# Two convolution tiles more as TensorE products, their shifted copies by way of main memory, and the convolution's projections ahead of the index scores

## The chip, the cores and the metric

The kernel runs on one core of a Trainium2 chip. The metric is the device time of one launch in microseconds (us). Engines are named as the profile names them: PE is TensorE (PEld its weight loads), DVE is VectorE, ACT is ScalarE, POOL is GpSimd, SP issues DMAs. Each runs its own stream of instructions in order and meets the others at semaphores.

## The reference, cut to what matters

The program has a first block of two layers and a second block. Only the first block's code changes. One of its layers is

```python
proj = jnp.einsum('bld,de->ble', h, w_in[l])
a, g, zc, q, k, v, za, qi, ki, wi = jnp.split(proj, IN_SPLITS, axis=-1)
y_conv = conformer_conv_branch(a, g, zc, ...)      # u = a * sigmoid(g); depthwise conv of 31 taps;
                                                   # layer norm; silu; times silu(zc)
y_attn = dsa_sparse_attention(rope(q), rope(k), v, rope(qi), rope(ki), wi, topk) * silu(za)
h = layer_norm(alpha * h + concat(y_conv, y_attn) @ w_out[l])
```

The sequence has 512 positions and 16 meta tokens in front (528 in all), the model 1024 features, and the convolution 512 channels. The sparse attention first makes an index score of every query with every key: the relu of eight heads' dot products, weighted and added up. Of each query's scores it keeps the 132 largest (a quarter of 528), and attends to those keys alone. The second block (windowed attention, gated linear attention, 16 experts) follows on the first block's output.

## The kernel before, in words

**Tiles.** A projection tile makes 128 output features for all positions: 48 matmuls of 264 columns (eight slices of the model, three products of high and low halves, two column halves) into a PSUM tile `pp` with two buffers. ACT makes the high half of the weights (`wh`, L160), DVE the low half (`wl`, L161). The convolution's channels are four tiles c = 0 to 3. `p_ag(c)` projects a and g of such a tile, ACT makes the tanh (`th`, L363), and DVE multiplies and adds into `u` (L364).

**Two ways to do the 31 taps of a tile.** A tile in `pconv` goes tap by tap: ACT multiplies the shifted `u` by a channel's weight into `prod` (L325, two buffers), and POOL adds it to `cv` (L327). Any other tile goes through `conv_products`: PE builds a table of the taps, DVE spreads it into the weights `cwt` (L339), 16 DMAs of SP copy `u`, shifted by 0 to 3 positions, into two SBUF buffers `us` (L344), and PE then does 128 matmuls of 32 rows (two bursts, L253 and L259) into a `pp` tile, which ACT moves to `cv`. Before, layer 0 has tiles 0, 1 and 2 tap by tap and 3 as products; layer 1 has 0 and 1 tap by tap and 2 and 3 as products.

**Scores and top-k.** `p_scores` has PE make the dot products (`pidx`, L242 and L243), ACT the relu (`rl`, L424), and DVE the weighted sums (`acc`, L428): 32 for each layer, of 128 to 512 columns. Top-k is DVE's alone: for three of the four query tiles it finds the eight largest of each row (MAX8, L440) and strikes them out (MATCH_REPLACE8, L441), 17 rounds a tile. The result is a mask that attention adds to its scores (`smb`, L624). The tag `rl` has three buffers, which `rl` and `th` share. The tag `sm` has two, which `us` and `smb` share.

**What sets the order.** Every phase is emitted at a priority level. `self.plan` holds for each layer the levels from first to last, the order of the phases (`seq`) and `pconv`. A scheduler with a timeline of its own turns this into one fixed stream for each engine when the program is built. Nothing is reordered on the chip.

Of the kernel before, what the change touches and what calls it, by code (L numbers as in the profile page):

```python
# [8 lines left out]
F32 = mybir.dt.float32  # L9
# [13 lines left out]
L = S + NM  # L23
KT = D // 128
W31 = 31
PAD = W31
CQ = 4
# [42 lines left out]
class Net:  # L70
    def __init__(self, tc, I, out, dbg=None, upto=99):
        self.tc, self.nc, self.I, self.out, self.dbg = tc, tc.nc, I, out, dbg
        self.upto = upto
        self.bgq = []
        self.plan = [
            (('w', 'topk', 'tail', 'idx', 'proj', 'conv', 'att', 'ag', 'rest', 'fill'),
             ('ag0', 'idx', 'q', 'k', 'sc', 'v', 'ag2', 'ag3', 'topk', 'ag1', 'zc', 'att', 'za'),
             (2, 0, 1, 3),
             (2, 3, 1, 0),
             (0, 1, 2)),  # L80
            (('w', 'tail', 'idx', 'conv', 'proj', 'att', 'ag', 'topk', 'rest', 'fill'),
             ('idx', 'q', 'k', 'sc', 'ag1', 'v', 'ag0', 'ag3', 'topk', 'ag2', 'att', 'za', 'zc'),
             (2, 0, 1, 3),
             (2, 3, 1, 0),
             (0, 1)),
        ]
        self.order2 = ('w', 'crit', 'att', 'gla', 'main', 'late', 'fill')
        self.gn0, self.apull, self.gpull, self.ng = 2, 3, (1, 0, 2, 1), 0
        self.early = ("qk", "qk", "u", "szc", "cv", "qi", "xl", "xl", "parts", "v", "c1", "sm", "sm", "one", "raw", "raw", "raw", "hw", "hl")
        self.last = ("raw", "u", "szc", "qi")  # L90
        self.cycle = ("qk", "qk", "u", "szc", "cv", "qi", "xl", "xl", "v", "sm", "sm", "one", "raw", "raw", "raw", "hw", "hl")
        self.piece = 264
        self.swap = True
        self.stack = True
        self.sqsum, self.sqe, self.xlp = 'v', 'AAAAAAAA', ()
        self.pairs2 = False
        self.pairs, self.spare = False, None
        self.cur = None
        self.pos = 0
# [173 lines left out]
    def layer(self, l):  # L273
        nc, I = self.nc, self.I
        w_in, w_out = I["w_in"][l], I["w_out"][l]
        hT = self.hT
        q0 = 0 if l == 0 else NM
        T = L - q0
# [7 lines left out]
        order, seq, tseq, sseq, pconv = self.plan[l]  # L286
# [27 lines left out]
        u = self.sb([128, 4, PAD + L], "u")  # L314
# [5 lines left out]
        def conv_tap(c, j):  # L320
            src = u[:, c, j + 1 + q0:j + 1 + q0 + T]
            if not prod:
                prod.append(self.sb([128, 2, L], "prod", "zM"))
            pr = prod[0][:, j % 2, :T] if j else cv[:, c, :]
            nc.scalar.activation(pr, src, AF.Identity, scale=taps[:, c, j + 1:j + 2], bias=0.0 if j else cvec[:, c, 31:32])  # L325
            if j:
                nc.gpsimd.tensor_tensor(cv[:, c, :], cv[:, c, :], pr, op=ALU.add)  # L327

        def conv_products(c):
            n = T // 2
            nx = T + W31 + 1 - CQ
            pt = self.ps([128, 4, 8], "pcv")
            for g in range(4):
                for k in range(CQ):
                    nc.tensor.matmul(pt[32 * k:32 * k + 32, g, :], self.ident[:, 32 * g:32 * g + 32], taps[:, c, k::CQ], start=True, stop=True)
            w = self.sb([128, 4, 8, 32], "cwt", "k2l")
            nc.vector.tensor_tensor(w.rearrange("p g e c -> p (g e) c"), self.mask32[:, None, :].to_broadcast([128, 32, 32]),  # L339
                                    pt.rearrange("p g e -> p (g e)")[:, :, None].to_broadcast([128, 32, 32]), op=ALU.mult)  # L340
            us = [self.sb([128, 2, nx], "us", "sm", 2) for _ in range(2)]
            for g in range(4):
                for k in range(CQ):
                    nc.sync.dma_start(us[g // 2][32 * k:32 * k + 32, g % 2, :], u[32 * g:32 * g + 32, c, k + q0:k + q0 + nx])  # L344
            ps = self.ps([128, 2, 512], "pp", "pp", 2)
            for k in range(2):
                products = []
                for e in range(8):
                    for g in (3, 2, 1, 0):
                        x0 = CQ * e + n * k  # L350
                        products.append(((ps[32 * g:32 * g + 32, k, :n], w[:, g, e, :], us[g // 2][:, g % 2, x0:x0 + n]),
                                         dict(start=e == 0, stop=e == 7, skip_group_check=True)))
                self.burst(products)
            nc.scalar.activation(cv[:, c, :].rearrange("p (k n) -> p k n", k=2), ps[:, :, :n], AF.Identity, scale=1.0, bias=cvec[:, c, 31:32])

        def p_ag(c):
            self.go("ag")
            ps = []
            for n in ("a", "g"):
                raw = self.load_w(w_in, WCOL[n] + 128 * c, 128)  # L360
                ps.append(self.proj(self.split_w(raw), 128, hT, KT, fsegs))
            th = self.sb([128, L], "th", "rl", 3)
            nc.scalar.activation(fseg(th), ps[1], AF.Tanh, scale=0.5)  # L363
            nc.vector.scalar_tensor_tensor(fseg(u[:, c, PAD:]), fseg(th), 1.0, ps[0], op0=ALU.add, op1=ALU.mult)  # L364
            self.go("conv")
            if c not in pconv:
                conv_products(c)
                return
            for j in range(W31):
                conv_tap(c, j)  # L370

# [110 lines left out]
        v = self.sb([128, 4, 512], "v")  # L482
# [195 lines left out]
        def p_zc():  # L678
            self.go("rest")
            for e, ps in self.proj_tiles(w_in, WCOL["zc"], 512, hT, KT, qsegs):  # L680
                tmp = self.sb([128, T], "th", "rl", 3)
                self.silu2(seg(szc[:, e, :]), ps, seg(tmp))

        phases = dict(ag0=lambda: p_ag(0), ag1=lambda: p_ag(1), ag2=lambda: p_ag(2), ag3=lambda: p_ag(3), idx=p_idx, sc=p_scores, topk=p_topk, k=p_k, q=p_q, v=p_v, att=p_att, za=p_za, zc=p_zc)
        for n in seq:
            phases[n]()

# [12 lines left out]
        for t in range(nt):  # L700
            ps = self.ps([128, 512], "tp")
            for c in range(4):
                nc.tensor.transpose(ps[:tw, c * 128:(c + 1) * 128], cv[:, c, t * tw:(t + 1) * tw], self.ident)
            x = self.sb([128, 512], "xct", "pT" if t < 4 else "rl", 4 if t < 4 else 3)
# [56 lines left out]
        sc = self.sb([128, 5, 2], "sc")  # L761
# [1007 lines left out]
```

## Time and profile before

| | us |
|---|---|
| median of 3 runs (lowest, highest) | 1878.74 (1877.99, 1878.78) |
| profiled execution, its time | 1881.06 |
| profiled execution, its span | 1879.3 |
| PE busy | 1692.2 |
| DVE busy | 928.1 |
| ACT busy | 773.4 |
| POOL busy | 221.1 |

The span is the trace's own length. The time of the same execution holds 1.8 us more, which lies outside the trace. Layer 0 runs from the start to about 400 us, layer 1 to about 785 us, and the second block from there on. All stretches below are counted from the start of the span.

### The profile page before, as it was taken

What the parts mean: (1) busy time and instruction counts of PE and PEld (TensorE: products, weight loads), DVE (VectorE), ACT (ScalarE), POOL (GpSimd) and SP (SyncE); (2) the same over time, 40 slices, a digit from 0 to 9 for tenths busy, and PEclk for the clock granted to TensorE, in tenths of its full rate; (3) what the DMA queues carried; (4) which work ended last, traced back from release to release, by engine and by line L of the source; (5) the groups of instructions that cost most, each with busy time, mean ns of one, the idle gap of its engine ahead of it and who ended that gap; (6) DMA issues with size and microseconds to landing.
All of it is one profiled execution on the core that took longest, in us unless ns stands there. A gap on an engine that the chain in (4) does not pass through costs nothing.

```text
span 1879.3 us, 29068 instructions
## 1 busy us (share of the span) xinstructions
PE 1692.2 (90%) x11947; PEld 1343.8 (72%) x11947; DVE 928.1 (49%) x1860; ACT 773.4 (41%) x1320; POOL 221.1 (12%) x161
## 2 busy tenths in 40 slices
PE   6989699889996698899999999999899998888888
PEld 6989598879985697889988889999633332233246
DVE  3899655567993246686533446543502221022054
ACT  3874576457665346445454544322300000000036
POOL 1621771000089000000000000000000000000000
PEclk9989899889997899999998999999899999999999
DMA  6213211122222211232202337656799999999971
GB/s 191 68 46 91 58 58 46 30 70 67 68 79 73 66 46 39 62 112 78 70 23 85 92 113 249 194 175 231 267 421 420 420 420 421 421 420 420 419 279 46
DMA packets 149414, 326.79 MB, mean 174 GB/s; under 512 B 13802, under 2 KB 103594, under 8 KB 130976
## 3 DMA queue, kind: packets, MB, share of 16 engines
q1 hardware_dynamic: 144416, 313.89, 45.4%
q10 hardware_dynamic: 3856, 7.37, 1.1%
q0 software_dynamic: 1008, 3.67, 0.5%
q8 instruction: 94, 1.54, 0.3%
q14 instruction: 40, 0.33, 0.1%
HBM read 305.22 MB, written 16.25 MB: 171 GB/s over the span
## 4 chain that ended last, share of the span: by engine, by line
PE 65%; DMA 15%; DVE 10%; ACT 5%; issue 2%; POOL 1%; SPq 1%; ACTq 0%; DVEq 0%; POOLq 0%
PE pp L182 39%; PE pp L1619 8%; DMA rawe<-in_w_exp_gate 6%; DMA rawe<-in_w_exp_down 5%; DMA rawe<-in_w_exp_up 4%; PE pp L1679 2%; DVE wl L161 2%; POOL cv L327 1%; SPq L344 1%; PE pp L259 1%; DVE acc L441 1%; PE tp L594 1%; PE pidx L253 1%; PE po L253 1%; DVE m L440 1%
## 5 line engine op out<-in xcount | busy, mean ns | idle before, releaser
L327 POOL TENSOR_TENSOR cv<-cv,prod 128x528 f32<-128x528 f32 (+1 forms) x150 | 214.2, 1428 | 396.6 <-ACT prod L325 387.8
L1619 PE MATMUL pp<-rawe,xf 128*64 128x512 f32 x1024 | 248.1, 600 | 14.1 <-DMA rawe<-in_w_exp_gate 9.6
L160 ACT CAST wh<-raw 128x1024 fp32r<-128x1024 f32 (+2 forms) x149 | 151.0, 1017 | 241.4 <-PE pp L182 216.0
L182 PE MATMUL pp<-hTh,wh 128*128 128x264 f32 (+2 forms) x1056 | 225.4, 291 | 18.2 <-ACT th L363 7.3
L161 DVE TENSOR_TENSOR wl<-raw,wh 128x1024 fp32r<-128x1024 f32 (+2 forms) x149 | 187.3, 1257 | 91.5 <-ACT wh L160 85.1
L182 PE MATMUL pp<-hTl,wh 128*128 128x264 f32 (+2 forms) x1056 | 220.8, 289 | 0.0
L182 PE MATMUL pp<-hTh,wl 128*128 128x264 f32 (+2 forms) x1056 | 219.7, 287 | 0.0
L1619 PEld LDWEIGHTS pp<-rawe,xf 128*64 128x64 f32 x1024 | 78.5, 137 | 158.5 <-issue 128.5
L182 PEld LDWEIGHTS pp<-hTh,wh 128*128 128x128 f32 (+1 forms) x1056 | 166.7, 190 | 25.7 <-ACT th L363 9.3
L182 PEld LDWEIGHTS pp<-hTl,wh 128*128 128x128 f32 (+1 forms) x1056 | 165.9, 190 | 4.4 <-issue 3.7
L182 PEld LDWEIGHTS pp<-hTh,wl 128*128 128x128 f32 (+1 forms) x1056 | 165.9, 190 | 2.8 <-issue 2.4
L182 PE MATMUL pp<-xTh,wh 128*128 128x264 f32 (+1 forms) x752 | 154.3, 286 | 2.9 <-ACT op L1048 2.3
L182 PE MATMUL pp<-xTl,wh 128*128 128x264 f32 (+1 forms) x752 | 155.8, 286 | 0.8 <-DVE xTl L1143 0.8
L182 PE MATMUL pp<-xTh,wl 128*128 128x264 f32 (+1 forms) x752 | 155.3, 284 | 0.0
L1619 PE MATMUL pp<-rawe,hid 128*64 128x512 f32 x512 | 126.4, 609 | 19.4 <-DMA rawe<-in_w_exp_down 19.0
L325 ACT ACTIVATE prod<-u,taps 128x528 f32<-128x528 f32 (+1 forms) x150 | 107.7, 729 | 57.2 <-POOL cv L327 55.6
L1476 POOL DMA_INDIRECT xr<-xrows,slots x7 | 6.7, 961 | 1037.1 <-DVE xf L1456 742.0
L1508 DVE SCALAR_TENSOR_TENSOR Y<-pp,per,Y 128x512 fp32r<-128x512 f32 x16 | 12.0, 749 | 233.2 <-ACT Y L1507 233.2
L182 PEld LDWEIGHTS pp<-xTh,wh 128*128 128x128 f32 (+1 forms) x752 | 115.7, 190 | 4.6 <-ACT op L1048 2.5
L182 PEld LDWEIGHTS pp<-xTl,wh 128*128 128x128 f32 (+1 forms) x752 | 115.8, 190 | 4.2 <-issue 3.0
L182 PEld LDWEIGHTS pp<-xTh,wl 128*128 128x128 f32 (+1 forms) x752 | 116.0, 190 | 0.8 <-issue 0.8
L1619 PEld LDWEIGHTS pp<-rawe,hid 128*64 128x64 f32 x512 | 39.1, 140 | 100.7 <-issue 61.6
(515 smaller groups left out, 2933.1 us busy)
## 6 DMA issues: line engine op xcount, KB each, us to landing
rawe<-in_w_exp_gate SPq DMA_DIRECT2D x53, 1024.0 KB, 16.2
rawe<-in_w_exp_up SPq DMA_DIRECT2D x52, 1024.0 KB, 15.0
rawe<-in_w_exp_down SPq DMA_DIRECT2D x51, 1024.0 KB, 19.5
raw<-in_w_in SPq DMA_DIRECT2D x45, 1024.0 KB, 5.4
rawe<-in_w_exp_down SPq DMA_DIRECT2D x26, 512.0 KB, 15.6
rawe<-in_w_exp_up SPq DMA_DIRECT2D x22, 512.0 KB, 16.4
rawe<-in_w_exp_gate SPq DMA_DIRECT2D x22, 512.0 KB, 17.3
raw<-in_w_in SPq DMA_DIRECT2D x20, 512.0 KB, 5.1
```

The source lines that it names most:

```text
L160: nc.scalar.copy(wh, raw_view)
L161: nc.vector.tensor_sub(wl, raw_view, wh.bitcast(F32))
L182: nc.tensor.matmul(ps[:m, s, x:min(x + k, n)], a[:, t, :m], b[:, c0 + x:min(c0 + x + k, c1)], start=(t == 0 and pi == 0 and x == 0), stop= ...
L253: first = self.nc.tensor.matmul(*args, **kw)
L259: self.nc.tensor.matmul(*args, **kw)
L325: nc.scalar.activation(pr, src, AF.Identity, scale=taps[:, c, j + 1:j + 2], bias=0.0 if j else cvec[:, c, 31:32])
L327: nc.gpsimd.tensor_tensor(cv[:, c, :], cv[:, c, :], pr, op=ALU.add)
L344: nc.sync.dma_start(us[g // 2][32 * k:32 * k + 32, g % 2, :], u[32 * g:32 * g + 32, c, k + q0:k + q0 + nx])
L440: nc.vector.max(m8, acc)
L441: nc.vector.match_replace(acc, m8, acc, NEG_MARK)
L1619: nc.tensor.matmul(ps[a, s, :], x[:, a], r, start=(t == 0 and k == 0), stop=(t == KT - 2 and k == 1), skip_group_check=True)
L1679: nc.tensor.matmul(ps[k][:, k, :], a[:, t, :], wp[t][:, w, k * 512:(k + 1) * 512], start=(t == 0 and pi == 0), stop=(t == KT - 1 and pi == 2))
```

## The change

`conv_products` is cut in two. `conv_operands`, which `p_ag` calls right behind `u`, makes the weights `cwt`, copies the tile's `u` to a tensor `ud` in main memory with one DMA, and reads it back with eight DMAs (one for each column half and shift) into `us`, of which each buffer now holds one column half of all channels. `conv_products` keeps the matmuls, as phases of their own (`cp1`, `cp2`, `cp3`) at the level of the projections. `pconv` loses one tile in each layer, so that 90 taps go tap by tap (150 before), and five of the eight tiles are products (three before). In layer 0 the phase `ag3` moves ahead of the scores, `ag1` behind them, and `ag2` to just ahead of `cp2`. In layer 1 `ag2` and `ag0` move ahead of the scores.

```diff
-             ('ag0', 'idx', 'q', 'k', 'sc', 'v', 'ag2', 'ag3', 'topk', 'ag1', 'zc', 'att', 'za'),
+             ('ag0', 'idx', 'q', 'k', 'ag3', 'sc', 'ag1', 'v', 'cp3', 'ag2', 'cp2', 'topk', 'zc', 'att', 'za'),
...
-             (0, 1, 2)),
+             (0, 1)),
...
-             ('idx', 'q', 'k', 'sc', 'ag1', 'v', 'ag0', 'ag3', 'topk', 'ag2', 'att', 'za', 'zc'),
+             ('idx', 'q', 'k', 'ag2', 'ag0', 'sc', 'cp2', 'ag1', 'v', 'cp1', 'ag3', 'cp3', 'topk', 'att', 'za', 'zc'),
...
-             (0, 1)),
+             (0,)),
...
+        def conv_operands(c):
             n = T // 2
-            nx = T + W31 + 1 - CQ
+            nx = n + W31 + 1 - CQ
...
-            us = [self.sb([128, 2, nx], "us", "sm", 2) for _ in range(2)]
-            for g in range(4):
+            us = [self.sb([128, 4, nx], "us", "sm", 2) for _ in range(2)]
+            ud = self.dram.tile([128, PAD + L], F32, name=f"ud{l}{c}")
+            nc.sync.dma_start(ud, u[:, c, :])
+            for h in range(2):
                 for k in range(CQ):
-                    nc.sync.dma_start(us[g // 2][32 * k:32 * k + 32, g % 2, :], u[32 * g:32 * g + 32, c, k + q0:k + q0 + nx])
+                    x0 = k + q0 + n * h
+                    nc.sync.dma_start(us[h][32 * k:32 * k + 32], ud.rearrange("(g p) x -> p g x", g=4)[:, :, x0:x0 + nx])
+            ready[c] = w, us
+
+        def conv_products(c):
+            self.go("proj")
+            n = T // 2
+            w, us = ready.pop(c)
...
         def p_ag(c):
-            self.go("ag")
+            self.go("ag" if c in pconv else "proj")
...
+            if c not in pconv:
+                conv_operands(c)
+                return
             self.go("conv")
-            if c not in pconv:
-                conv_products(c)
-                return
```

The order that the scheduler makes of it is shown at three places. The first is DVE in layer 0, where the first score sums (`acc<-rl`) stand. Before, they stand between the rope rows (`qk`, `sw`) of the q and k tiles:

```order
L217 TENSOR_TENSOR qk<-pp,c_72 128x528
L218 TENSOR_TENSOR sw<-sw,c_72 128x528
L414 TENSOR_TENSOR rm<-rm,ws 128x128
L219 TENSOR_TENSOR qk<-qk,sw 128x528
L415 TENSOR_REDUCE acc<-rm 128x16
L428 SCALAR_TENSOR_TENSOR acc<-rl,ws,c_72 128x384
L428 SCALAR_TENSOR_TENSOR acc<-rl,ws,acc 128x384
L161 TENSOR_TENSOR wl<-raw,wh 128x1024
```

Now the last rope stands ahead of all of them, and so do the weights and the `u` (L375) of tile c = 3:

```order
L217 TENSOR_TENSOR qk<-pp,c_72 128x528
L218 TENSOR_TENSOR sw<-sw,c_72 128x528
L219 TENSOR_TENSOR qk<-qk,sw 128x528
L161 TENSOR_TENSOR wl<-raw,wh 128x1024 x2
L375 SCALAR_TENSOR_TENSOR u<-th,pp 128x528
L439 SCALAR_TENSOR_TENSOR acc<-rl,ws,c_72 128x384
L439 SCALAR_TENSOR_TENSOR acc<-rl,ws,acc 128x384 x7
```

The score sums have moved behind the k tiles that were still to come and the two projection tiles of c = 3. Layer 1 is alike: there the `u` of tiles 2 and 0 stand ahead of the first `acc`.

The second place is the end of layer 0's top-k on DVE, where the `u` of the last product tile (c = 2) now stands. Rows L451 and L452 are the rounds of top-k:

```order
L161 TENSOR_TENSOR wl<-raw,wh 128x1024
L451 MAX m_2373<-acc 128x8
L375 SCALAR_TENSOR_TENSOR u<-th,pp 128x528
L452 MATCH_REPLACE acc<-m_2336,acc 128x276
L560 TENSOR_REDUCE mxm<-smm 16x8
L452 MATCH_REPLACE acc<-m_2373,acc 128x532
L451 MAX m_2336<-acc 128x8
```

It stands behind 45 of the 51 rounds. SP issues that tile's copies behind it; the store waits for DVE, and the first load waits for the store and, with its buffer, for PE:

```order
L345 DMA ud_2207<-u 128x559 [waits DMAHW5_49,DVE_49]
L349 DMA us<-ud_2207 32x4x292 [waits DMAHW6_49,DMAHW5_49,PE_49]
L349 DMA us<-ud_2207 32x4x292 [waits DMAHW7_49]
L349 DMA us<-ud_2207 32x4x292 [waits DMAHW0_49]
L349 DMA us<-ud_2207 32x4x292 [waits DMAHW1_49]
L349 DMA us<-ud_2207 32x4x292 [waits DMAHW2_49,PE_49]
```

One store and eight loads stand where 16 copies stood. The third place is PE at the same point of layer 0:

```order
L571 MATMUL po<-vM,ptm_2655 16x512
L586 MATMUL psm<-kmb,qk 128x32 x4
L253 MATMUL pidx<-qk 128x384
L259 MATMUL pidx<-qk 128x384
L253 MATMUL pp<-us,cwt 32x264
L259 MATMUL pp<-us,cwt 32x264 x31
L253 MATMUL pidx<-qk 128x384
L259 MATMUL pidx<-qk 128x384
L605 MATMUL tp<-base,smb 128x128 x6
L182 MATMUL pp<-hTh,wh 128x264 x2
```

(The two bursts of `pp<-us` read alike; the second is left out.) The products of c = 2 are the last work ahead of attention, and all projection tiles but those of zc and za have been moved ahead of them. Before, the two tiles of `ag1` stood behind the products too. The streams of the second block are nearly the same in both programs.

## Rows read from the trace of the kernel before

**Rows 1.** Waits of PE, 0 to 330 us: total, times, longest.

```profile
PE pp L253 <- ACT prod L325: 15.4, 1, 15.4
PE pp L182 <- DVE qk L217: 6.4, 2, 5.0
```

**Rows 2.** Waits of PE, 480 to 700 us.

```profile
PE pp L253 <- DMA us<-u: 32.3, 2, 17.9
PE pp L182 <- ACT th L363: 5.9, 2, 3.0
```

**Rows 3.** Windows: length, busy of PE, PEld, DVE, ACT, POOL, granted clock, DMA.

```profile
81.40:130.00 48.60, 42.78 (x297) 41.43 (x297) 47.99 (x69) 37.13 (x66) 19.48 (x12) 0.89 0.15 44
130.00:196.60 66.60, 65.35 (x539) 60.96 (x537) 63.87 (x167) 30.07 (x51) 12.24 (x9) 1.00 0.32 88
196.60:212.00 15.40, 0.00 (x0) 0.00 (x0) 14.53 (x35) 9.21 (x13) 13.07 (x10) 0.59 0.31 74
212.00:221.50 9.50, 9.46 (x129) 8.36 (x129) 1.21 (x1) 4.54 (x7) 8.95 (x8) 0.77 0.01 2
221.50:313.00 91.50, 90.73 (x796) 82.52 (x794) 47.74 (x138) 68.06 (x144) 48.18 (x35) 1.00 0.18 59
440.00:499.30 59.30, 59.30 (x477) 58.63 (x476) 55.60 (x106) 44.61 (x78) 0.00 (x0) 1.00 0.22 63
499.30:511.00 11.70, 10.87 (x90) 10.66 (x88) 11.26 (x30) 5.15 (x11) 0.00 (x0) 1.00 0.17 46
571.30:589.20 17.90, 0.01 (x1) 0.04 (x2) 6.17 (x5) 10.21 (x15) 16.86 (x13) 0.60 0.45 126
612.30:626.60 14.30, 0.00 (x0) 0.00 (x0) 1.84 (x2) 1.32 (x2) 0.00 (x0) 0.62 0.41 105
626.60:635.10 8.50, 8.44 (x128) 7.50 (x128) 0.00 (x0) 0.00 (x0) 0.00 (x0) 0.84 0.02 4
635.10:712.00 76.90, 76.90 (x702) 70.13 (x699) 37.22 (x129) 41.24 (x102) 0.00 (x0) 1.00 0.17 56
```

**Rows 4.** Timeline of DVE, 84 to 85 us and 199 to 222 us.

```profile
84.03 1.39 DVE L428 SCALAR_TENSOR_TENSOR acc<-rl,ws,c 128x384 f32<-128x384 f32 x1
...
199.65 0.69 DVE L364 SCALAR_TENSOR_TENSOR u<-th,pp 128x528 f32<-128x528 f32 x1
...
206.43 0.09 DVE L441 MATCH_VALUE_LOAD acc<-m,acc 128x8 f32 x1
...
208.49 0.09 DVE L441 MATCH_VALUE_LOAD acc<-m,acc 128x8 f32 x1
...
221.58 0.62 DVE L624 CUSTOM_DVE_ANT_0 smb<-pidx,acc,mi 128x384 f32<-128x384 f32 x1 [8.37 <-PE pp L259]
```

**Rows 5.** Timeline of SP, 199 to 222 us: start, length, what it issues.

```profile
200.37 10.01 SPq L344 DMA_DIRECT2D us<-u  x16
```

**Rows 6.** The tile `us`: time from issue to landing of its DMAs.

```profile
DMA to landing us min/median/max: 2.0/2.0/2.0
```

**Rows 7.** Timeline of DVE in layer 1: first sum, and the `u` behind top-k.

```profile
451.67 0.61 DVE L428 SCALAR_TENSOR_TENSOR acc<-rl,ws,c 128x384 f32<-128x384 f32 x1
...
576.78 0.69 DVE L364 SCALAR_TENSOR_TENSOR u<-th,pp 128x528 f32<-128x528 f32 x1
```

**Rows 8.** The page's costliest groups: the taps on POOL and ACT.

```profile
L327 POOL TENSOR_TENSOR cv<-cv,prod 128x528 f32<-128x528 f32 (+1 forms) x150 | 214.2, 1428 | 396.6 <-ACT prod L325 387.8
L325 ACT ACTIVATE prod<-u,taps 128x528 f32<-128x528 f32 (+1 forms) x150 | 107.7, 729 | 57.2 <-POOL cv L327 55.6
```

**Rows 9.** The tile `h1d` (second block, SBUF to main memory): issue to landing of 256 KB.

```profile
DMA to landing us min/median/max: 2.5/2.5/2.5
```

**Rows 10.** DVE by shapes, 84.03 to 213.3 us: busy, mean ns, idle before.

```profile
L161 DVE TENSOR_TENSOR wl<-raw,wh 128x1024 fp32r<-128x1024 f32 x15 | 19.2, 1282 | 3.1 <-ACT wh L160 2.8
L440 DVE MAX8 m<-acc 128x8 f32<-128x404 f32 x17 | 9.7, 571 | 0.0
L428 DVE SCALAR_TENSOR_TENSOR acc<-rl,ws,acc 128x384 f32<-128x384 f32 x7 | 7.3, 1040 | 0.3
```

**Rows 11.** Timeline of DVE, 84 to 104.5 us: one sum in its two lengths.

```profile
85.52 0.62 DVE L428 SCALAR_TENSOR_TENSOR acc<-rl,ws,acc 128x384 f32<-128x384 f32 x1
...
89.48 1.68 DVE L428 SCALAR_TENSOR_TENSOR acc<-rl,ws,acc 128x384 f32<-128x384 f32 x1
```

**Rows 12.** DVE by shapes in layer 1, 451.67 to 574.7 us.

```profile
L440 DVE MAX8 m<-acc 128x8 f32<-128x404 f32 x17 | 9.8, 575 | 0.0
L428 DVE SCALAR_TENSOR_TENSOR acc<-rl,ws,acc 128x384 f32<-128x384 f32 x7 | 4.3, 615 | 0.1
```

**Rows 13.** Windows of the tile `pidx` alone, end of layer 1's k tiles.

```profile
440.00:499.30 59.30, 12.83 (x64) 9.18 (x64) 0.00 (x0) 11.45 (x22) 1.00 0.22 63
```

More of the change, by code (lines that the diff above doesn't have):

```diff
@@ L76, in __init__ @@
             (('w', 'topk', 'tail', 'idx', 'proj', 'conv', 'att', 'ag', 'rest', 'fill'),
-             ('ag0', 'idx', 'q', 'k', 'sc', 'v', 'ag2', 'ag3', 'topk', 'ag1', 'zc', 'att', 'za'),
-             (2, 0, 1, 3),
-             (2, 3, 1, 0),
-             (0, 1, 2)),
-            (('w', 'tail', 'idx', 'conv', 'proj', 'att', 'ag', 'topk', 'rest', 'fill'),
-             ('idx', 'q', 'k', 'sc', 'ag1', 'v', 'ag0', 'ag3', 'topk', 'ag2', 'att', 'za', 'zc'),
+             ('ag0', 'idx', 'q', 'k', 'ag3', 'sc', 'ag1', 'v', 'cp3', 'ag2', 'cp2', 'topk', 'zc', 'att', 'za'),
              (2, 0, 1, 3),
@@ L85, in __init__ @@
              (0, 1)),
+            (('w', 'tail', 'idx', 'conv', 'proj', 'att', 'ag', 'topk', 'rest', 'fill'),
+             ('idx', 'q', 'k', 'ag2', 'ag0', 'sc', 'cp2', 'ag1', 'v', 'cp1', 'ag3', 'cp3', 'topk', 'att', 'za', 'zc'),
+             (2, 0, 1, 3),
+             (2, 3, 1, 0),
+             (0,)),
         ]
@@ L327, in conv_tap @@
                 nc.gpsimd.tensor_tensor(cv[:, c, :], cv[:, c, :], pr, op=ALU.add)
-        def conv_products(c):
+        ready = {}
+        def conv_operands(c):
             n = T // 2
-            nx = T + W31 + 1 - CQ
+            nx = n + W31 + 1 - CQ
             pt = self.ps([128, 4, 8], "pcv")
@@ L349, in conv_products @@
                     for g in (3, 2, 1, 0):
-                        x0 = CQ * e + n * k
-                        products.append(((ps[32 * g:32 * g + 32, k, :n], w[:, g, e, :], us[g // 2][:, g % 2, x0:x0 + n]),
+                        x0 = CQ * e
+                        products.append(((ps[32 * g:32 * g + 32, k, :n], w[:, g, e, :], us[k][:, g, x0:x0 + n]),
                                          dict(start=e == 0, stop=e == 7, skip_group_check=True)))
@@ L682, in p_zc @@
                 self.silu2(seg(szc[:, e, :]), ps, seg(tmp))
-        phases = dict(ag0=lambda: p_ag(0), ag1=lambda: p_ag(1), ag2=lambda: p_ag(2), ag3=lambda: p_ag(3), idx=p_idx, sc=p_scores, topk=p_topk, k=p_k, q=p_q, v=p_v, att=p_att, za=p_za, zc=p_zc)
+        phases = dict(cp1=lambda: conv_products(1), cp2=lambda: conv_products(2), cp3=lambda: conv_products(3), ag0=lambda: p_ag(0), ag1=lambda: p_ag(1), ag2=lambda: p_ag(2), ag3=lambda: p_ag(3), idx=p_idx, sc=p_scores, topk=p_topk, k=p_k, q=p_q, v=p_v, att=p_att, za=p_za, zc=p_zc)
         for n in seq:
```

## Prediction

> **What bounds the kernel now.** I read PE's waits first, since PE is busiest. In the first block three waits stand out, all in front of the products of a convolution tile. One is 15.4 us in layer 0 [rows 1], and two are 32.3 us together in layer 1 [rows 2]: 17.9 and 14.3 us by the windows [rows 3]. That is 47.6 us in which PE does nothing at all. The view names ACT `prod` for the first, but the matmuls read `us`, so I follow the copies.
>
> In layer 0, DVE makes `u` of tile 3 at 199.65 [rows 4], SP spends 10.01 us issuing the 16 copies [rows 5], the last lands 2.0 us later [rows 6], and the products start at 212.0 [rows 3]. So the copy leg is 11.7 us behind `u`'s end, and only the rest is lateness of `u` itself. `u` is late because DVE is full: 63.87 of 66.6 us and 14.53 of 15.4 us in the windows ahead [rows 3]. Its work there is the score sums and top-k, from 84.03 in layer 0 [rows 4] and from 451.67 in layer 1 [rows 7] to the `u` behind top-k at 576.78 [rows 7]. After the products PE is full again (90.73 of 91.5, 76.90 of 76.9, clock 1.00 [rows 3]). So **DVE sets when the last products start, and PE everything after them.** A shift of that point should carry through to the end, because the second block's streams hardly differ.
>
> **The change, part by part.** *Taps.* Sixty taps fewer are 60 x 1.43 = 86 us of POOL and 60 x 0.73 = 44 us of ACT [rows 8]. Neither engine sets a stage's end, so I count this at nothing by itself. What it is worth is DVE's time beside POOL (below).
>
> *Products.* Two more tiles at 8.5 to 9.5 us each [rows 3]. They stand in the stretch in which PE would otherwise wait for the last `u`; that wait hides them. Where it is gone, they cost about 8 us each.
>
> *Copy leg.* The trace has no store of `u`. The nearest row is `h1d`, 2.5 us to landing for 256 KB [rows 9]; the store is 286 KB, so 2.6. Eight loads issue at about 0.6 us each (10.01 / 16 [rows 5]), some 4.6 us, and the last lands after 2.0 [rows 6] to 2.5 us. Sum 9.4 us against 11.7; bounds 8 and 14. By the Trainium skill's "DMA: Bandwidth & Descriptors" (Anatomy of one DMA), a transfer is some 2.0 us plus its bytes at 436 GB/s. For the store and 1.2 MB of loads that would give an estimated 7.4 us, and a total 4 us lower than mine. The rows have the loads' issue as the longer part, so I keep 9.4.
>
> *Order, layer 0.* At 81.4 six q and k tiles are left. Two tiles take 11.7 us [rows 3], so these six and the two of `ag3` take 46.8, and with two early score products PE is done at 129. Tanh and `u` take 2: the sums start at 131 instead of 84. From there the order has on DVE, up to `u` of tile 2:
> - 46 rounds of top-k. A round of each of two tiles takes 208.49 - 206.43 = 2.06 us [rows 4], so 1.03 each: 47.4.
> - 8 `wl` at 1.28 [rows 10]: 10.2.
> - 32 sums. Alone, one of 384 columns takes 0.53 (the next instruction starts 0.53 behind it [rows 11]; busy reads 0.615 [rows 12]); over 128 to 512 columns I take 0.46: 14.7.
> - `qis`, three `u`, `cwt` and small ones: about 10.
>
> That is 82 us, so `u` ends at 213 if POOL costs nothing. Tile 1's taps run beside the rounds; a handful of two-input operations then pay 0.4 to 1.1 us each (below): 2 to 9, I take 4. So: `u` at 217, copies 226.4, products of 9.5 us [rows 3] to 235.9. The like point of before is 221.5, plus the 11.7 of `ag1`, which PE still had to do then: 233.2. **Layer 0: +2.7 us.** PE has `ag3`, `ag1`, `ag2` and all of v behind it by about 210, and would wait 16 us.
>
> *Order, layer 1.* The k tiles end at 499.3 before. The score products among them (12.83 us busy, overlaps included [rows 13]) now come later; I take 10, so 489. Two pairs of projection tiles (23.4 us) and a wait for the tanh (3.0 [rows 2]) bring 515.5, and `u` of tile 0 ends at 517.5, where the sums now start: 66 us later than 451.67. DVE's list up to `u` of tile 3 is that of layer 0 with one more `cwt` and round: 83 us, to 600.5.
>
> Here, though, tile 0's taps stand between the relus on ACT, so POOL adds beside the sums. What that costs is the open term. With POOL adding (19.48 of 48.6 us [rows 3]) a sum of 384 columns took 1.040 us [rows 10], without it (POOL 0.00 in layer 1's window [rows 3]) 0.615 [rows 12]: +0.43 on average, and 1.06 at worst (1.68 against 0.62 [rows 11]). MAX8 took 571 and 575 ns [rows 10, 12], so top-k does not pay. By the order 44 two-input operations lie in that stretch: 44 x 0.43 = 19 us. The bounds are nothing, and one full 1.1 for each of 30 adds, 33 us. I take 19, the mean row. So: `u` at 619.5, copies 629, products of 8.5 us to 637.5; before 635.1, with the same work behind. **Layer 1: +2.4 us.** PE would be through with the rest at about 600 and wait 29 us.
>
> **Sum.** +5 us; the profiled execution's 1881.06 becomes 1886.2, and the median of 1878.74, which lies 2.3 below it, becomes 1884. PE's waits are moved, not removed: 16 + 29 = 45 against 47.6. DVE gets less work beside its sums, but starts them 47 and 66 us later, and idles in between (some 3.5 of each 5.85 us tile is work).
>
> **Rivals.**
> 1. *POOL's adds cost DVE nothing there*, since ACT spreads the taps. `u` comes at 213 and 600.5. Layer 0 gives -1.3. In layer 1 PE itself, ready at about 600, sets the end near 620 (-15). Total -16: **1862**. For it: MAX8 rows are the same with and without POOL. Against it: 0.43 us on the same sum [rows 10, 12].
> 2. *Every add meets a sum.* The sums alternate with relus and taps on ACT, so POOL is busier than when [rows 10] were taken. Layer 1 pays 33 instead of 19, layer 0 9 instead of 4: +19 more, **1903**. It decides once POOL is busy for over two thirds of the stretch. The Trainium skill's "GPSIMD Engine Reference" (Specifications) has VectorE share SBUF interfaces with GpSimd, with contention for instructions with two SBUF inputs; by that all 44 would be exposed. The trace agrees in kind (sums pay, MAX8 doesn't) and gives the price.
> 3. *The way by main memory is slow*: store and loads in series at 14 us instead of 9.4. On the path twice, +9: **1893**.
> 4. *It cancels*: layer 1 pays 15 instead of 19, and the total is within 3.8 us of before.
>
> **How the numbers follow.** Within 0.2% (3.8 us) is what a measurement here can't tell from no change. The summed case, from 1877 to 1892 by the copy leg and half of the POOL term, has 0.50, and rival 4 is its lower part: 0.20 same, 0.24 slower, 0.06 faster. Rival 1 has 0.27 (faster), rival 2 0.13, rival 3 0.10 (slower both). So 0.33 faster, 0.20 same, 0.47 slower. The range leaves out 0.1 on each side: 1862 to 1898.
>
> **What would show it.** In the profile after: no PE wait for `us` between the layers' v tiles and two of about 16 and 29 us ahead of `cp2` in layer 0 and `cp3` in layer 1. The first `acc` at 131 and about 517. DVE with idle time ahead of them and hardly any behind. The sums of layer 1 at about 1 us each while POOL adds. Store to last load some 9 us. If the sums there take 0.6, rival 1 holds; if `u` of tile 3 comes after 632, rival 2. A first `acc` that doesn't wait for `u`, or a wait of PE for something else than `us` in attention behind the products, would make the forecast wrong in kind.

## The result, and the profile after

| | before | changed |
|---|---|---|
| median, us (lowest to highest, 4 runs each) | 1878.76 (1877.99 to 1881.56) | 1903.2 (1902.02 to 1905.7) |
| ratio (95% interval) | | 1.0131 (1.0119 to 1.0144) |
| profiled execution: span | 1879.3 | 1903.9 |

The change costs 24.4 us. The forecast was slower, at 1884 and no later than 1898. The sign was right and the size was not.

PE's waits from 60 to 700 us of the changed kernel, the three longest (total, times, longest):

```profile
PE pp L182 <- ACT th L374: 24.6, 4, 11.4
PE psm L567 <- ACT smm L562: 14.6, 1, 14.6
PE pp L253 <- DMA us<-ud: 5.3, 1, 5.3
```

The long waits for `us` of before [rows 1, 2] are gone by name only: the three groups here are 44.5 us against 47.7. The matmuls that now wait stand ahead of the products in PE's stream, and what they wait for (a tanh, a row of the meta tokens' attention) passes through ACT, and through DVE, behind the same queue of sums and top-k. ACT's timeline shows it for the tanh that the longest wait for `th` is about. It waits 4.30 us for a sum itself, since `th` and `rl` share their buffers:

```profile
578.08 0.61 ACT L374 ACTIVATE th<-pp 128x528 f32<-128x528 f32 x1 [4.30 <-DVE acc L439]
```

A view of waits names the first instruction that stops, not the one that the stretch was planned around.

So the next view is DVE's own timeline. These rows are of the changed kernel: the last `u` ahead of layer 0's sums, the first sum, the last `u` of layer 0, the start of layer 1, and layer 1's first sum and last `u`.

```profile
132.52 0.70 DVE L375 SCALAR_TENSOR_TENSOR u<-th,pp 128x528 f32<-128x528 f32 x1
133.13 0.61 DVE L439 SCALAR_TENSOR_TENSOR acc<-rl,ws,c 128x384 f32<-128x384 f32 x1
...
223.72 0.68 DVE L375 SCALAR_TENSOR_TENSOR u<-th,pp 128x528 f32<-128x528 f32 x1
...
401.07 0.16 DVE L316 MEMSET u<- 128x124 f32 x1
...
527.52 0.61 DVE L439 SCALAR_TENSOR_TENSOR acc<-rl,ws,c 128x384 f32<-128x384 f32 x1
...
634.23 0.68 DVE L375 SCALAR_TENSOR_TENSOR u<-th,pp 128x528 f32<-128x528 f32 x1
```

The sums start at 133.1 where they started at 84.0 [rows 4], and at 527.5 where they started at 451.7 [rows 7]. From the first sum to the end of the last `u` DVE takes 91.3 us in layer 0 and 107.4 in layer 1. Why layer 1 takes more shows in DVE's groups by shape, 527.5 to 575 us (busy, mean ns, idle before):

```profile
L439 DVE SCALAR_TENSOR_TENSOR acc<-rl,ws,acc 128x512 f32<-128x512 f32 x7 | 8.0, 1143 | 0.0
L439 DVE SCALAR_TENSOR_TENSOR acc<-rl,ws,acc 128x384 f32<-128x384 f32 x7 | 7.3, 1049 | 3.4 <-ACT rl L435 3.0
...
L451 DVE MAX8 m<-acc 128x8 f32<-128x404 f32 x8 | 4.6, 572 | 0.1
L161 DVE TENSOR_TENSOR wl<-raw,wh 128x1024 fp32r<-128x1024 f32 x2 | 4.6, 2286 | 0.0
```

A sum of 384 columns takes 1049 ns. It took 615 in the same layer of before, where POOL was idle at that point [rows 12]. MAX8 is unmoved at 572 ns. POOL adds for 33.46 of these 47.5 us (of the whole 107.4 it is 41.95), which the window's row shows (length, then busy of PE, PEld, DVE, ACT, POOL):

```profile
527.50:575.00 47.50, 35.65 (x320) 30.70 (x312) 43.86 (x63) 31.77 (x55) 33.46 (x24) 0.85 0.04 12
```

The way by main memory itself is short. SP's timeline, and PE's for the first product behind each (the last product tile of each layer):

```profile
224.42 0.35 SPq L345 DMA_DIRECT2D ud<-u  x1
227.16 3.66 SPq L349 DMA_DIRECT2D us<-ud  x8
...
634.94 0.35 SPq L345 DMA_DIRECT2D ud<-u  x1
637.52 3.64 SPq L349 DMA_DIRECT2D us<-ud  x8
```

```profile
232.42 0.65 PE L253 MATMUL pp<-us,cwt 128*32 128x264 f32 x1
...
642.17 0.61 PE L253 MATMUL pp<-us,cwt 128*32 128x256 f32 x1 [5.30 <-DMA us<-ud]
```

From `u`'s end to the first product is 8.0 and 7.3 us. Before it was 11.7. In layer 0 PE has no wait for `us` ahead of the product, so there the 8.0 us are an upper bound for the copies.

**Where the 24.6 us between the spans lie.** Layer 1 starts at 401.07; before it was 392.03: 9.0 us. The first store of `h1d`, at the start of the second block, is issued at 813.1 against 796.6, so layer 1 adds 7.5. The second block adds the remaining 8.1 (1090.8 against 1082.7).

### The profile page after: what moved, and what is told of

Read it like the earlier page. It is cut to its first block, busy times and chain, and to the rows that moved or that the text cites. A ratio compares the mean times of both kernels' runs of the same rounds, so it can differ in the third digit from the quotient of the medians.

```text
span 1903.9 us, 29578 instructions
## 1 busy us (share of the span) xinstructions
PE 1720.2 (90%) x12267; PEld 1350.1 (71%) x12267; DVE 942.7 (50%) x1862; ACT 732.5 (38%) x1260; POOL 136.6 (7%) x101
## 4 chain that ended last, share of the span: by engine, by line
PE 42%; DMA 21%; DVE 6%; ACT 3%; issue 1%; SPq 0%; ACTq 0%; DVEq 0%
PE pp L182 26%; DMA rawe<-in_w_exp_down 7%; DMA rawe<-in_w_exp_up 6%; DMA rawe<-in_w_exp_gate 6%; PE pp L1630 4%; PE pp L1690 2%; DMA rawe<-in_w_ple_gate 1%; DVE acc L439 1%; PE pp L259 1%; PE po L253 1%; DVE acc L452 1%; PE pa L1042 1%; DVE m L451 1%; PE tp L963 0%; DVE wl L161 0%
## 5 line engine op out<-in xcount | busy, mean ns | idle before, releaser
L327 POOL TENSOR_TENSOR cv<-cv,prod 128x528 f32<-128x528 f32 (+1 forms) x90 | 129.7, 1441 | 457.4 <-ACT prod L325 452.7
L1512 ACT COPY hid<-tp 128x512 f32<-128x512 f32 x16 | 8.7, 589 | 186.8 <-PE tp L1510 186.8
```

## The experiments

The theory after the result: (a) the sums start late because two or four more projection tiles, and with them the k tiles still to come, stand ahead of them; (b) POOL's adds then meet the sums; (c) more product tiles and the way by main memory are not what costs. The rivals: the product tiles cost it, or main memory, or DVE's list is simply longer than was summed. All medians are in us; where a ratio stands, it is to before on the same chip, with its 95% interval.

### e1, the scores first again

```diff
-             ('ag0', 'idx', 'q', 'k', 'ag3', 'sc', 'ag1', 'v', 'cp3', 'ag2', 'cp2', 'topk', 'zc', 'att', 'za'),
+             ('ag0', 'idx', 'q', 'k', 'sc', 'ag3', 'ag1', 'v', 'cp3', 'ag2', 'cp2', 'topk', 'zc', 'att', 'za'),
-             ('idx', 'q', 'k', 'ag2', 'ag0', 'sc', 'cp2', 'ag1', 'v', 'cp1', 'ag3', 'cp3', 'topk', 'att', 'za', 'zc'),
+             ('idx', 'q', 'k', 'sc', 'ag2', 'ag0', 'cp2', 'ag1', 'v', 'cp1', 'ag3', 'cp3', 'topk', 'att', 'za', 'zc'),
```

> The changed kernel with one thing put back: in both layers the scores (sc) stand right behind the k tiles again, ahead of the projections ag3 (layer 0) and ag2, ag0 (layer 1). Theory (the loss comes from the score sums that start 49 and 76 us later, so that DVE is late with the last u): sums start at about 84 and 452 us; the last u comes near 208 in layer 0 and near 604 in layer 1, where TensorE itself is only just ready; total about 1862, 40 us below the changed kernel and some 15 below the kernel before. Rival (the two more product tiles or the way by main memory are what costs): 1895 or more.

Measured: **1858.81**, ratio 0.9908 (0.9892 to 0.9925). That is 44 us below the changed kernel and 18 below the one before, from moving one word in each list. DVE's timeline has the sums at their old places, and the last `u` of layer 1 41 us earlier:

```profile
83.05 1.39 DVE L439 SCALAR_TENSOR_TENSOR acc<-rl,ws,c 128x384 f32<-128x384 f32 x1
...
213.50 0.69 DVE L375 SCALAR_TENSOR_TENSOR u<-th,pp 128x528 f32<-128x528 f32 x1
...
448.49 0.61 DVE L439 SCALAR_TENSOR_TENSOR acc<-rl,ws,c 128x384 f32<-128x384 f32 x1
...
593.68 0.70 DVE L375 SCALAR_TENSOR_TENSOR u<-th,pp 128x528 f32<-128x528 f32 x1
```

Part (a) holds: the order is the loss. Everything else in the change, taken together and in this order, is a gain.

### e2 and e5, the taps left out, late sums and early sums

```diff
-            for j in range(W31):
+            for j in range(1):
                 conv_tap(c, j)
```

e2 makes this edit in the changed kernel, e5 in e1. The convolution of the tap-by-tap tiles is left out but for one tap. ACT's multiplications go with POOL's adds, and the scheduler makes its order anew.

> The changed kernel without 30 of the 31 taps of its three tap-by-tap tiles (only the first is done, so those tiles' convolution is left out), order otherwise as the scheduler makes it. Theory (GpSimd's adds stretch VectorE's sums: 24 us in layer 1, 9 in layer 0): from the first sum to the last u 82 to 84 us in both layers instead of 107 and 91; total 1870 to 1880. Rival (VectorE's list is simply longer than was summed, GpSimd costs it little): 1895 or more.

> The kernel with the scores first (1858.8) without 30 of the 31 taps of its three tap-by-tap tiles (those tiles' convolution is left out). Theory (adds on GpSimd cost time only where TensorE waits for VectorE; with the scores first that is 6.4 us at the q and k tiles and 6.3 us at the meta attention): 8 to 12 us less, 1847 to 1851. Rival (the adds cost VectorE, and so the kernel, the same in any order, 35 us as in the changed kernel): about 1824.

Measured: e2 **1867.77** (0.9949, 0.9933 to 0.9966), e5 **1844.14** (0.9814, 0.9798 to 0.9831). e2's rows on DVE:

```profile
128.88 0.61 DVE L439 SCALAR_TENSOR_TENSOR acc<-rl,ws,c 128x384 f32<-128x384 f32 x1
...
211.75 0.68 DVE L375 SCALAR_TENSOR_TENSOR u<-th,pp 128x528 f32<-128x528 f32 x1
...
514.85 0.61 DVE L439 SCALAR_TENSOR_TENSOR acc<-rl,ws,c 128x384 f32<-128x384 f32 x1
...
599.65 0.68 DVE L375 SCALAR_TENSOR_TENSOR u<-th,pp 128x528 f32<-128x528 f32 x1
```

From first sum to the end of the last `u` it is 83.5 and 85.5 us, 7.7 and 21.9 less than in the changed kernel. In layer 0 both stretches hold the same 212 instructions, and DVE's busy time makes the difference (82.35 against 90.06 us): the adds cost 7.7 us there, and another 4.2 ahead of the first sum (128.9 against 133.1). In layer 1 the stretches differ in more than the adds. The scheduler put the last `u` of e2 behind 43 MAX8 of top-k, and that of the changed kernel behind 48. These are the windows and the MAX8 groups that differ, of the changed kernel and then of e2:

```profile
527.52:634.91 107.39, 86.20 (x800) 76.22 (x790) 103.75 (x215) 48.80 (x82) 41.95 (x30) 0.88 0.21 60
L451 DVE MAX8 m<-acc 128x8 f32<-128x532 f32 x15 | 10.4, 692 | 0.0
L451 DVE MAX8 m<-acc 128x8 f32<-128x276 f32 x16 | 6.9, 432 | 0.0
```

```profile
514.85:600.33 85.48, 79.65 (x800) 71.26 (x790) 79.40 (x198) 30.51 (x52) 0.00 (x0) 0.96 0.27 75
L451 DVE MAX8 m<-acc 128x8 f32<-128x532 f32 x13 | 9.0, 695 | 0.0
L451 DVE MAX8 m<-acc 128x8 f32<-128x276 f32 x13 | 5.7, 435 | 0.0
```

The rounds more are some 6 us, and DVE idles 3.6 us in the first and 6.1 in the second. Instructions that stand in both, compared by shape, are about 19 us longer in the changed kernel, 14 of it in the sums: that is the toll of the 30 adds there. It is in the length of DVE's own instructions and not in waits for ACT, so ACT's multiplications are not what costs. In layer 1 of before a sum took 615 ns with ACT busy for 44.61 of 59.3 us and POOL idle [rows 3, 12].

The four medians make a table (the chips differ by run; before has medians from 1876.5 to 1878.8 on them):

| | with taps | without | difference |
|---|---|---|---|
| sums late (changed, e2) | 1903.2 | 1867.8 | 35.4 |
| sums early (e1, e5) | 1858.8 | 1844.1 | 14.7 |
| difference | 44.4 | 23.6 | |

So late sums alone cost some 24 us. The other 21 of the 44 come only where both are there: with late sums DVE is what PE waits for, so all of the adds' toll shows, and they stand beside layer 1's sums as well (7.7, 4.2 and 19 us). e5 came out 3 us lower than expected, e2 2 us below its range.

### e6, only layer 1's taps moved behind the sums

```diff
...
+                own = self.sb([128, 8, NM], "own", "rm", 2).rearrange("p h k -> p (h k)")[:, :W31 + 1]
+                nc.vector.scalar_tensor_tensor(own, accs[0][:, NM:NM + W31 + 1], 0.0, taps[:, c, :], op0=ALU.mult, op1=ALU.add)
...
```

The tap weights come from this copy, which also reads the sums, so ACT and POOL can't start the tile ahead of them.

> The changed kernel with layer 1's one tap-by-tap tile started only when the score sums are through (its tap weights come from a copy that depends on the last sum); all else as in the changed kernel. Theory (22 us of layer 1's loss are adds that meet score sums): first sum to last u 107 us becomes 85 to 92, total 1884 to 1889. Rival (the adds cost as much beside top-k, or it is only the late start): 1900 or more.

Measured: **1882.72**, ratio 1.0027 (1.0016 to 1.0037), 20.5 below the changed kernel with the same work done. Its groups by shape, 527.2 to 575 us:

```profile
L448 DVE SCALAR_TENSOR_TENSOR acc<-rl,ws,acc 128x512 f32<-128x512 f32 x7 | 5.2, 739 | 0.0
L448 DVE SCALAR_TENSOR_TENSOR acc<-rl,ws,acc 128x384 f32<-128x384 f32 x7 | 4.3, 619 | 1.2 <-ACT rl L444 0.8
```

First sum (527.27) to the end of the last `u` (614.93 + 0.69) is 88.4 us, with 44 MAX8 in it. Part (b) holds. By shape against e2, 30 adds cost about 19 us beside the sums in the changed kernel, 0.6 us each, but 4.7 beside top-k here, 0.16 us each. The 4.7 us lie in `wl` and in the few operations that end a tile's top-k.

### e3 and e7, the copies alone

e3 gives the kernel before the way by main memory and nothing else; e7 gives e1 the 16 direct copies back. These are lines of e7's edit; e3 makes it the other way round.

```diff
-            ud = self.dram.tile([128, PAD + L], F32, name=f"ud{l}{c}")
-            nc.sync.dma_start(ud, u[:, c, :])
...
+            for g in range(4):
+                for k in range(CQ):
+                    nc.sync.dma_start(us[g // 2][32 * k:32 * k + 32, g % 2, :], u[32 * g:32 * g + 32, c, k + q0:k + q0 + nx])
```

> The kernel before with the way by main memory alone (one store, eight loads, a column half per buffer); order of phases and the tiles done as products as before. Theory (the copy leg is on the path three times, and it measures 7 to 8 us by main memory against 11.7 directly): three times 4 us less, about 1867. Rival (part of it is taken up by TensorE being busy or by other lateness): 1874 to 1879.

> The kernel with the scores first, but with the 16 direct copies of before in place of the way by main memory; products still as phases of their own. Theory (the copy leg is on the path once, ahead of layer 1's last products, where TensorE waits 5.7 us): 4 to 8 us more, 1863 to 1867. Rival (the way by main memory is what makes the scores-first kernel fast): 1870 or more. Second rival (it doesn't matter): 1859.

Measured: e3 **1874.02** (0.9977, 0.9964 to 0.9989), e7 **1877.58** (0.9999, 0.9989 to 1.0009). In e3 the first block ends 10.6 us sooner (`h1d` at 786.0 against 796.6), close to three times 4. The median shows only 3 of it and lies at the rival's end; the second block of the profiled execution took 1085.7 us against 1082.7, and the runs spread from 1865.8 to 1876.7.

e7 went to the rival: without main memory the whole gain of e1 is gone. The last leg of layer 1 in e7, on SP and on PE:

```profile
611.70 10.31 SPq L346 DMA_DIRECT2D us<-u  x16
```

```profile
623.60 0.61 PE L253 MATMUL pp<-us,cwt 128*32 128x256 f32 x1 [10.74 <-DMA us<-u]
```

`u` ends at 611.6, so this leg takes 12.0 us; in e1 (593.68 + 0.70 to 601.60) it is 7.2. I had counted it on the path once. PE waits at three of the five: 2.4 us in layer 0, 3.9 and 10.7 in layer 1; in e1 only one, 5.7. Of the 19 us some 13 are such longer legs (4.8 on the last, 3.7 in layer 0 and 4.1 on layer 1's first). The rest (slower products behind the added waits, loads of weights later on SP) I have not taken apart.

### e4 and e8, the number of product tiles

e4 is the kernel before with the change's `pconv` (first two pairs of lines); e8 is e1 with that of before and a list for layer 0 that goes with it (third pair; `cp1` leaves layer 1's).

```diff
-             (0, 1, 2)),
+             (0, 1)),
...
-             (0, 1)),
+             (0,)),
...
-             ('ag0', 'idx', 'q', 'k', 'sc', 'ag3', 'ag1', 'v', 'cp3', 'ag2', 'cp2', 'topk', 'zc', 'att', 'za'),
+             ('ag0', 'idx', 'q', 'k', 'sc', 'ag2', 'ag1', 'v', 'ag3', 'cp3', 'topk', 'zc', 'att', 'za'),
```

> The kernel before with five product tiles instead of three (the tiles of the change), the direct copies and the order of phases of before. Theory (each product tile at its old place stops TensorE for a copy leg of 11.7 us and costs 8.5 to 9.5 us of products, less what VectorE gains from 60 fewer adds): 1895 to 1915. Rival (fewer adds beside VectorE are worth more than that): 1879 or less.

> The kernel with the scores first, but with three product tiles as in the kernel before (c = 3 in layer 0, 2 and 3 in layer 1), 150 taps. Theory (with the scores first TensorE sets the end, and each product tile is 8.5 to 9.5 us of TensorE): 8 to 17 us less, 1842 to 1851. Rival (60 more adds stretch VectorE until TensorE waits for it again): 1859 or more.

Measured: e4 **1910.13** (1.0171, 1.0154 to 1.0188), e8 **1857.61** (0.9892, 0.9873 to 0.991). At the old place two product tiles more cost 33 us: PE's waits for `us` come to 68.2 us (23.4 in layer 0, 44.8 in layer 1) where they were 47.7 [rows 1, 2], and two tiles of products are another 17 to 19. Together that is more than the 33; the 60 adds fewer stand against it, and I have not taken them apart. As phases of their own with other work ahead, five cost the same as three within 1.2 us. My 8 to 17 us for two tiles of PE's work did not come through; e8's trace has PE waiting 10.1 us for `smm` in layer 0 where e1 waits 6.3, so part of it went into waits for ACT and DVE, which is the rival's way; the median lies between the two forecasts.

### e9 and e10, a version for use

e9 is e1 with layer 0's tile 0 started only behind that layer's sums, by the same two lines as e6; e10 is the same with three product tiles.

> The kernel with the scores first, with layer 0's tile 0 started tap by tap only when that layer's score sums are through (its tap weights come from a copy that depends on the last sum). Theory (adds cost VectorE up to 1.1 us where they meet score sums and ropes, and about 0.2 us beside top-k): of the 11 us that layer 0 gains without any taps, 6 to 9 come back; 1850 to 1853. Rival (the adds only move their cost into top-k): 1857 to 1861.

> The same with three product tiles instead of five (as in the kernel before). Theory (TensorE sets the end with the scores first, but 60 more adds then stand beside top-k and its last operations): about as fast as with five, 1848 to 1854. Rival (two tiles less of TensorE's products come through): 1840 or less.

Measured: e9 **1851.56** (0.9863, 0.9844 to 0.9882), e10 **1856.89** (0.9887, 0.987 to 0.9903). e9 beats both kernels, by 26 and 52 us. Its interval lies below e1's and overlaps with e10's. Its layer 1 starts at 384.11, e1's at 389.69: the 5.6 us are where they were expected, a little under the 6 to 9. e10 came out above its range, and the two intervals do not tell five tiles from three.

### e11 and e12, the same two kernels profiled again

> The changed kernel unaltered, profiled a second time. If the 8 us that its second block took longer than before's belong to that one execution, the block takes some 1080 to 1086 us from its first store of h1d to the end; if they belong to the kernel (when it arrives, and with which clock), 1089 to 1092 again.

> The kernel before unaltered, profiled a second time: 1082 to 1084 us for the same stretch if it belongs to the kernel, anything from 1079 to 1091 if to the execution.

One execution each: 1896.15 and 1876.84. The first block repeats: `h1d` at 812.1 and 795.4, 16.7 us apart (16.5 the first time). The second block does not. It takes 1082.2 us in e11 against 1090.8, and 1079.6 in e12 against 1082.7. So only some 2.6 of its 8.1 us repeat, and the rest does not belong to the instruction streams, as far as one more execution of each, on another chip, can tell.

## Why the prediction was wrong, by its own steps

- **What bounds the kernel: right.** DVE set the end of both stages, PE what follows. No run spoke against it, and e1 shows that the places where the sums start decide.
- **Sums start late: right in time.** 131 predicted, 133.1 measured; in layer 1 125.5 us behind the layer's start predicted (517.5 less 392.0), 126.5 measured. In layer 0 two errors meet in that: without adds it is 128.9, and the adds put 4.2 on it.
- **POOL's toll: failed in layer 0, by size.** I took 4 us. Measured are 7.7, plus 4.2 ahead of the sums that I left at nothing, because I took the tiles there at PE's pace (46.8 us, from a row in which POOL is idle). In layer 1 I took 19, and about 19 are measured (e2, by shape). The mean row held: POOL was busy 40% of the time in it, and 39% of layer 1's stretch (41.95 of 107.4).
- **DVE's list: right in layer 0, too short in layer 1.** 82 us against 83.5 (e2). In layer 1 I took 83, but 107.4 less the 19 of toll are some 88.5. Of that DVE idles 3.6, nearly all of it where sums wait for ACT's relu, which I left at nothing. e2's 85.5 looks nearer only because five rounds fewer stand in it.
- **Rival 2's total was luck.** It gave 1903, with a toll of 42 us where about 31 are measured. Layer 1 paid 19, not 33, and the rest of the total came from the list and from the second block. Its sign came too, `u` of tile 3 behind 632 (it ends at 634.9), but layer 1 had started 9.0 us later than before; counted from that start it is 625.9.
- **Copy leg: too dear.** 9.4 predicted, 7.3 measured, and at most 8.0 in layer 0. The eight loads issue in 3.65 us, not 4.6. The 7.4 us worked out from the Trainium skill's "DMA: Bandwidth & Descriptors" was nearer; the trace agrees with it here within 0.6 us. That section fits its formula to DMAs that GpSimd issues, though, and these are SP's.
- **Products hidden in the wait: likely, not tested in the changed order.** PE still waits 14.6 us (`smm`) and 5.3 us (`us`) behind the other product tiles there. In the better order five and three come within 1.2 us (e8), where three also have 60 more adds.
- **"A shift carries through to the end": failed by 8 us.** The second block added 8.1 in the first two profiles, and about 2.6 in e11 against e12.
- **So the steps that failed** are POOL's toll in layer 0 (4 us for 11.9), DVE's list and its waits in layer 1 (83 for 88.5), and the second block (nothing for 8.1). The first block was forecast at +5 and came out at +16.5 (9.0 and 7.5): the first two terms were 13 us short and the cheaper copies gave 3 back, which is 10 of the 11 us between them.
- **The marks to look for:** I asked for waits for `us` of 16 and 29 us. The waits came, but under `smm` and `th`. The price was on the right engine and the name was wrong, because I listed what stands behind the product and not what stands ahead of it.

**The second block's 8.1 us.** The streams are not quite the same there. PE comes to the first transpose of `xr` sooner in the changed kernel (564.6 us behind the first store of `h1d`, against 579.4) and waits for its DMA, 2.58 us here and 2.23 in e11. Both executions of before have no such wait. That is about the size of what repeats, and over all profiles here the eight with such a wait take 1084.8 us for the second block on average, the six without 1081.6. No run changes this wait alone. The changed kernel, then before:

```profile
1377.66 0.30 PE L1494 MATMUL tp<-base,xr 128*128 128x128 f32 x1 [2.58 <-DMA xr<-xrows,slots]
```

```profile
1376.00 1.09 PE L1483 MATMUL tp<-base,xr 128*128 128x128 f32 x8
```

The rest stays open. It lies at two places where PE's clock differs, as the windows of the two first profiles show (length, busy of PE, PEld, DVE, ACT, POOL, granted clock; of the changed kernel, then the same work of before):

```profile
1007.05:1047.05 40.00, 40.00 (x243) 34.94 (x242) 11.75 (x21) 18.57 (x27) 0.00 (x0) 0.82 0.28 81
...
1047.00:1082.30 35.30, 32.97 (x226) 29.56 (x225) 14.33 (x27) 17.49 (x24) 0.00 (x0) 0.95 0.24 75
1082.30:1110.80 28.50, 26.18 (x179) 23.86 (x178) 12.50 (x23) 13.87 (x19) 0.00 (x0) 0.94 0.24 77
...
1822.40:1854.84 32.44, 27.97 (x112) 15.32 (x109) 9.58 (x15) 4.87 (x8) 0.00 (x0) 0.89 0.56 217
```

```profile
990.00:1030.00 40.00, 40.00 (x242) 35.23 (x241) 11.76 (x21) 18.56 (x27) 0.00 (x0) 0.82 0.28 83
...
1030.00:1064.00 34.00, 31.67 (x226) 28.22 (x227) 14.23 (x27) 17.48 (x24) 0.00 (x0) 1.00 0.25 78
1064.00:1091.00 27.00, 24.68 (x179) 22.36 (x178) 12.55 (x23) 13.91 (x19) 0.00 (x0) 1.00 0.26 81
...
1800.00:1830.00 30.00, 26.58 (x116) 13.50 (x113) 9.61 (x15) 4.88 (x8) 0.00 (x0) 1.00 0.60 233
```

In the second and third row of each the same instructions take 63.8 us at 0.95 and 0.94, and 61.0 at 1.00: 2.8 us. In the last row it is 32.4 us at 0.89 against 30.0 at 1.00, 1.4 of the 2.4 in PE's busy time. At 1.00 the clock is at its level of 2.4 GHz throughout; a lower figure is a mean with some of the stretch at 1.2. In the 40 us ahead of the second row PE was busy without a gap in both kernels, at a mean of 0.82 in both, so these rows do not tell what decides it, and no run here tried it.

## What to carry to other kernels

Before work is moved ahead on the engine that waits, look at what the other engine's queue starts with: here two and four projection tiles (12 and 23 us of matmuls) put ahead of the scores made the first sums start 49 and 67 us later in their layers, and took the head start from the engine that the end of the stage waits for. An add on GpSimd had no price of its own here; it cost what it met, 0.6 us beside two-input sums and 0.16 to 0.26 beside top-k (e6, and layer 0's 7.7 us for 30), so when it ran mattered more than how many there were. And a version is best judged by its parts: the change as made was 1.3% slower, and the same change with one word moved in each list 0.9% faster.

## What the runs showed that was not expected

- Eight DMAs from main memory behind one store (7.2 to 8.3 us from `u` to the last tile's first product) beat 16 direct copies (11.7 to 12.0). Issue on SP makes the difference: 3.65 us for 8 of 32 partitions by 4 x 292, 0.46 each, against 10.0 to 10.3 for 16, 0.63 to 0.64 each. The first load starting 2.5 to 3.2 us behind the store takes part of it back.
- The second block, with nearly the same instructions, took 1079 to 1091 us over the profiles here (1079.4 in e4, 1090.8 in the changed kernel), so a comparison of single executions is good to some 10 us and no better. A wait of 1.0 to 3.2 us for `xr` is there in some of these kernels and not in others.
- Two-input work of VectorE beside GpSimd's adds took 1.05 us against 0.615 for a sum of 384 columns, and 2.29 us against 1.22 on average without adds (e2, layer 1) for `wl`, while MAX8 stayed at 572 ns. The Trainium skill's "GPSIMD Engine Reference" (Specifications) names instructions with two SBUF inputs as the ones that contend, which these rows bear out.
